# Inverse decay by a second scan and a Newton step, and one projection moved, in an RWKV-7 / HGRN-2 / attention trunk

## The chip, the cores and the metric

The kernel runs on one core of a Trainium2 chip. The metric is the device time of one execution in microseconds (us), as the median of several executions. The engines are named PE (TensorE, matrix products; PEld is its weight load), DVE (VectorE), ACT (ScalarE), POOL (GpSimd) and SP (SyncE, which here issues most DMAs). Each runs its own list of instructions in a fixed order and waits for the others through semaphores. SBUF is the on-chip memory that all of them read; PSUM is the small memory that PE writes its sums to.

## The reference

One layer of a hybrid trunk on 1024 tokens of width 1024, in fp32: a normed input projection `w_in`, three groups of heads (HGRN2, dilated window attention, RWKV-7), an output projection, a gated MLP with a short convolution, an embedding gate and a last norm. The change lies in RWKV-7 alone:

```python
w = -jax.nn.softplus(-(w0 + jnp.tanh(wd) @ w2)) - 0.5
decay = jnp.exp(-jnp.exp(w))          # = exp(-e^-0.5 * sigmoid(w0 + tanh(wd) @ w2))
a = jax.nn.sigmoid(a0 + ad @ a2)
kk = kk / jnp.maximum(jnp.linalg.norm(kk, axis=-1, keepdims=True), 1e-12)
k = k * (1.0 + (a - 1.0) * k_a)
# over the tokens t, per head of 64:
sa = state @ (-kk_t)
state = state * w_t + sa (kk_t * a_t)^T + v_t k_t^T
y_t = state @ r_t
```

The recurrence is computed in chunks of 64 tokens. Within a chunk `gam` is the running product of the decay and `ig` its inverse; r and kk are multiplied by `gam`, k and kk*a by `ig`, after which a chunk is a few matrix products and the inverse of a triangular matrix.

## The kernel before

Rows (partitions) are channels, columns are the 1024 tokens. A projection of 128 channels is 48 matmuls of 128x128 by 512 columns: 8 parts of the contraction, three products of high and low halves each (hi*hi, hi*lo, lo*hi, L137, L139, L141), two halves of the tokens. Its sum `dp` takes one of the **two** PSUM buffers of the pool `dps` (2 x 1024 columns). A third projection can start only when the first one's buffer has been read for the last time. Its weights come by DMA as `wraw`, ACT casts `whi` (L114), and POOL or DVE by turns subtracts `wlo` (L116).

There are 30 projections j. 0 to 7 are RWKV's (lora, gate, then k, r, v of head pair 0 as 2, 3, 4, of pair 1 as 5, 6, 7) and run through `proj` and `mix_in` (L492): scale `dp` in place by the norm (L320, DVE), copy on ACT (L501), mix with the previous token (L502, DVE). 8 and up belong to the other heads and are the **filling**: `project_rest` (L425) is a generator that issues 6 matmuls at each step, at a tile's end its finish (DVE scale L320 and ACT sigmoid L457 by halves, or one DVE product L454, into `zst`) and its store.

The heads are worked in two pairs p. For each:

- `rwkv_prep` (L537): k, its squares and norm (`kks`, `kr`), the LoRA products `lo`, sigmoids for w and a, an exp (L572), the scan for `gam` (L581), the reciprocal `ig` (L584), `ai`, r, `kkn`, `bhat`, `ar` (L609, L622), 8 or 6 filling steps, then `rwkv_scores` (PE `sc` L654, DVE `sc` L656), for pair 1 also v, then k with a, `khat` (POOL, L623), `bv`.
- `rwkv_inverse` (L660): 31 steps of two small DVE operations, `Tt` (L678) and `Tb` (L680), and DMAs that lay the result out as Tc and Uc. PE meanwhile does filling, v of pair 0, and the bonus `bon`; then it needs Tc for `py` (L790).
- `rwkv_main`: 22 slots of small matmuls (`px`, `pgm`, `pyo`, `pS`), one filling step in each; the state S passes from chunk to chunk by pS and DVE L903. `rwkv_norm` of the first half runs as a member of it (gnv, gnr on POOL, y times gnr, L764), of the second half behind it, with transposes `yt` (L770) and `pg`.

The order of the program text is not the order on the engines: the framework's scheduler orders the instructions of each engine by the dependencies and its own costs, and the buffers of the pools add waits. What stands below as the order is the built program's.

Of the kernel before, what the change touches and what calls it, by code (L numbers as in the profile page):

```python
# [18 lines left out]
P = 128  # L19
# [70 lines left out]
class Trunk:  # L90
# [334 lines left out]
    def project_rest(self, js):  # L425


        nc = self.nc
        w = None
        for i, j in enumerate(js):  # L430
            w = w or self.load_w(self.a["w_in"][j])
            ps = self.dps.tile([P, T], F32, tag="dp", name=self.nm("dp"))
            nxt = None
            for k in range(ND):
                self.mm3({0: ps[:, :HT], 1: ps[:, HT:]}, w(k), self.X[k], k == 0, k == ND - 1)
                if k == 3 and i + 1 < len(js):
                    nxt = self.load_w(self.a["w_in"][js[i + 1]])
                yield
            w = nxt
            t = self.keep.tile([P, T], F32, tag="zst", name=self.nm("zst"), bufs=2)  # L440
            kind = (j - 8) % 4 if j < 24 else 2
            parts = [(t, ps, self.R)]
            if j < 24 and kind < 3:
                parts = [(t[:, :HT], ps[:, HT:][:, ::-1], self.R[:, HT:][:, ::-1]), (t[:, HT:], ps[:, :HT], self.R[:, :HT])]
            for part in parts:
                self.finish(kind, *part)
            d = self.zpool.tile([P, T], F32, tag=f"z{j}", name=f"z{j}")
            nc.sync.dma_start(d, t)
            self.z[j] = d
        yield  # L450
# [55 lines left out]
    def rwkv(self):  # L506
# [7 lines left out]
        for p in (0, 1):  # L514
            d = {}
            lead, n = self.FILL[p]
            fill = self.project_rest([next(js) for _ in range(n)])
            with tc.tile_pool(name=f"pre{p}", bufs=1) as tp:
                self.rwkv_prep(p, tp, lt, d, fill)
                self.rwkv_inverse(p, tp, d)  # L520
# [16 lines left out]
    def rwkv_prep(self, p, tp, lt, d, fill):  # L537
# [6 lines left out]
        def col(c):  # L544
            return par[:, c + p:c + p + 1]
# [18 lines left out]
        for hf in (0, 1):  # L564
# [3 lines left out]
            nc.scalar.activation(w[:, sl], ps, AF.Sigmoid, bias=col(PC_W0))  # L568
            ps = mxp.tile([P, HT], F32, tag="mx", name=self.nm("lo"))
            nc.tensor.matmul(ps, par[64:128, PC_LORA + p * P:PC_LORA + (p + 1) * P], lt[64:128, sl], start=True, stop=True)  # L570
            nc.scalar.activation(a[:, sl], ps, AF.Sigmoid, bias=col(PC_A0))
        nc.scalar.activation(w, w, AF.Exp, scale=-EXP_M05)  # L572

        dz = tr("dz")
        w3 = w.rearrange("p (c i) -> p c i", i=64)
        dz3 = dz.rearrange("p (c i) -> p c i", i=64)
        nc.gpsimd.memset(dz, 0.0)
        nc.vector.tensor_copy(dz3[:, :, 0:1], w3[:, :, 0:1])
        nc.vector.memset(w3[:, :, 0:1], 0.0)
        gam = tr("gam")  # L580
        nc.vector.tensor_tensor_scan(gam, w, dz, 0.0, ALU.mult, ALU.add)  # L581
        ig = tr("ig")
        for hf in (0, 1):
            nc.vector.reciprocal(ig[:, hf * HT:(hf + 1) * HT], gam[:, hf * HT:(hf + 1) * HT])  # L584
        ai = tr("ai")
        nc.vector.tensor_tensor(ai, a, ig, ALU.mult)
        r = self.mix_in(3 + 3 * p, 0 + p, "r", tr)
# [21 lines left out]
            nc.vector.tensor_tensor(a4[:, :, :, 1:], k4[:, :, :, 1:], g4[:, :, :, :63], ALU.mult)  # L609
            nc.scalar.copy(a4[:, :, :, 0:1], k4[:, :, :, 0:1])  # L610
        d.update(ar=ar, be=be, kh=kh)
        for _ in range(6 if p else 8):
            next(fill)
        self.rwkv_scores(p, tp, d)
        if p:
# [115 lines left out]
    HALVES = tuple((slice(a, a + 32), slice(a + 32, a + 64)) for a in (0, 64))  # L731

    def rwkv_norm(self, p, sg, d, hf, fill, n):
        for i, _ in enumerate(self.rwkv_norm_steps(p, sg, d, hf)):
            for _ in range(2 if i < 4 else 1):
                for _ in range(1 if n == 3 else 2):
                    next(fill, None)

    def rwkv_norm_steps(self, p, sg, d, hf):

# [25 lines left out]
        yield  # L766
        yield
        pt = mxp.tile([P, HT], F32, tag="mx", name=self.nm("yt"))
        for m in range(4):
            nc.tensor.transpose(self.turned(pt[:, m * P:(m + 1) * P], m % 2), y[:, m * P:(m + 1) * P], self.ident)  # L770
        nc.vector.tensor_scalar(o, pt, col(PC_LNW), col(PC_LNB), ALU.mult, ALU.add)
        nc.vector.tensor_tensor(o, o, d["bv"][:, sl], ALU.add)
        pg = mxp.tile([P, HT], F32, tag="mx", name=self.nm("pg"))
# [1086 lines left out]
```

## Time and profile before

| | us |
|---|---|
| median of 3 executions | 1405.99 (1405.21 to 1406.52) |
| the profiled execution | 1404.77 |
| its span, first to last instruction | 1403.0 |
| PE busy in the span | 1375.7 |
| mean granted PE clock | 0.994 of full speed |

In the timeline a row is: start in us from the span's start, duration, engine, line, operation, out<-in, shapes, xcount (rows of one group in a row), and in brackets the idle time of the engine ahead of it with what ended it. A row of waits gives engine, what waited, <- what ended the wait: us in total, how often, the longest. A row of stretches gives the stretch, its length, the busy time (and count) of PE, PEld, DVE, ACT and POOL, the PE clock, the DMA share and GB/s. Pair 0's preparation runs from about 53 to 89 us, its inverse to 124, the first loop from 133 to 190, pair 1's preparation from 210 to 254, its inverse to 286, the second loop from there.

### The profile page before, as it was taken

What the parts mean: (1) busy time and instruction counts of PE and PEld (TensorE: products, weight loads), DVE (VectorE), ACT (ScalarE), POOL (GpSimd) and SP (SyncE); (2) the same over time, 40 slices, a digit from 0 to 9 for tenths busy, and PEclk for the clock granted to TensorE, in tenths of its full rate; (3) what the DMA queues carried; (4) which work ended last, traced back from release to release, by engine and by line L of the source; (5) the groups of instructions that cost most, each with busy time, mean ns of one, the idle gap of its engine ahead of it and who ended that gap; (6) DMA issues with size and microseconds to landing.
All of it is one profiled execution on the core that took longest, in us unless ns stands there. A gap on an engine that the chain in (4) does not pass through costs nothing.

```text
span 1403.0 us, 22344 instructions
## 1 busy us (share of the span) xinstructions
PE 1375.7 (98%) x8644; PEld 1116.5 (80%) x8644; DVE 1063.7 (76%) x1613; ACT 611.8 (44%) x1049; POOL 395.5 (28%) x287
## 2 busy tenths in 40 slices
PE   9999999999999999999999999999999999999997
PEld 6878777877878768788788888888888888888886
DVE  7696456835667796468889888888988799777685
ACT  7522323133255584255544343444344444455542
POOL 5411012101222242221345454545453000002342
PEclk9999999999999999999999999999999999999998
DMA  6123111321622212653232332332324963441443
GB/s 224 61 83 104 64 61 47 100 73 62 225 83 99 91 61 71 253 180 125 94 127 98 113 103 90 102 105 98 114 98 166 351 217 106 127 143 45 136 138 140
DMA packets 80122, 167.61 MB, mean 119 GB/s; under 512 B 19984, under 2 KB 22288, under 8 KB 80016
## 3 DMA queue, kind: packets, MB, share of 16 engines
q1 hardware_dynamic: 66784, 147.05, 31.3%
q10 hardware_dynamic: 12224, 15.47, 3.2%
q0 software_dynamic: 1008, 3.67, 0.7%
q8 instruction: 68, 1.11, 0.3%
q14 instruction: 38, 0.31, 0.1%
HBM read 119.76 MB, written 46.40 MB: 118 GB/s over the span
## 4 chain that ended last, share of the span: by engine, by line
PE 78%; DVE 8%; issue 8%; ACT 3%; POOL 3%; DMA 1%; SPq 0%; POOLq 0%; ACTq 0%; DVEq 0%
PE bg L1338 17%; PE bv L1338 13%; PE bv L1639 7%; PE bg L1639 7%; PE dp L137 7%; PE dp L139 7%; PE dp L141 7%; PE swq L1169 1%; DVE ig L584 1%; PE hsc L1015 1%; PE zp L137 1%; DVE xl L409 1%; PE zp L141 1%; PE zp L139 1%; PE swo L1209 1%
## 5 line engine op out<-in xcount | busy, mean ns | idle before, releaser
L137 PE MATMUL dp<-xh,whi 128*128 128x512 f32 x544 | 186.9, 406 | 1.2 <-DVE r L502 0.7
L139 PE MATMUL dp<-xl,whi 128*128 128x512 f32 x544 | 180.5, 394 | 0.6 <-DVE xl L409 0.5
L141 PE MATMUL dp<-xh,wlo 128*128 128x512 f32 x544 | 179.7, 392 | 0.0
L116 POOL TENSOR_TENSOR wlo<-wraw,whi 128x512 fp32r<-128x512 f32 x60 | 84.5, 1410 | 264.9 <-ACT whi L114 226.8
L116 POOL TENSOR_TENSOR wlo<-raw,whi 128x512 fp32r<-128x512 f32 x84 | 135.0, 1626 | 75.9 <-ACT whi L114 75.9
L114 ACT CAST whi<-wraw 128x512 fp32r<-128x512 f32 x120 | 72.9, 618 | 158.0 <-PE dp L139 103.0
L1338 PE MATMUL bg<-t,whi 128*128 128x512 f32 x352 | 133.4, 389 | 0.0
L139 PEld LDWEIGHTS dp<-xl,whi 128*128 128x128 f32 x544 | 102.3, 188 | 24.6 <-DVE xl L409 2.5
L141 PEld LDWEIGHTS dp<-xh,wlo 128*128 128x128 f32 x544 | 102.2, 188 | 23.8 <-issue 2.0
L137 PEld LDWEIGHTS dp<-xh,whi 128*128 128x128 f32 x544 | 98.8, 189 | 26.0 <-issue 3.9
L116 POOL TENSOR_TENSOR wlo<-s,whi 128x512 fp32r<-128x512 f32 x44 | 64.5, 1466 | 168.6 <-ACT whi L114 168.6
L1639 PE MATMUL bg<-t,whi 128*128 128x512 f32 x308 | 95.2, 390 | 0.0
L1639 PE MATMUL bv<-t,whi 128*128 128x512 f32 x308 | 94.8, 389 | 0.0
L114 ACT CAST whi<-raw 128x512 fp32r<-128x512 f32 x88 | 52.7, 620 | 93.7 <-issue 48.5
L114 ACT CAST whi<-s 128x512 fp32r<-128x512 f32 x66 | 38.9, 620 | 120.2 <-PE bg L1338 112.8
L1338 PEld LDWEIGHTS bg<-t,whi 128*128 128x128 f32 x352 | 66.1, 188 | 13.7
L190 POOL TENSOR_TENSOR rst<-rst,mhalf 128x4 f32<-128x4 f32 (+1 forms) x9 | 10.2, 1134 | 234.0 <-DVE rst L186 218.0
L1635 ACT CAST t<-t 128x512 fp32r<-128x512 f32 x77 | 47.8, 622 | 45.8 <-PE bv L1639 32.7
L1338 PE MATMUL bg<-t,wlo 128*128 128x512 f32 x176 | 67.5, 389 | 0.0
L1639 PEld LDWEIGHTS bv<-t,whi 128*128 128x128 f32 x308 | 57.8, 188 | 12.0
L1639 PEld LDWEIGHTS bg<-t,whi 128*128 128x128 f32 x308 | 57.8, 188 | 11.9
L116 DVE TENSOR_TENSOR wlo<-wraw,whi 128x512 fp32r<-128x512 f32 x60 | 48.2, 807 | 20.7 <-ACT whi L114 18.5
(417 smaller groups left out, 3423.6 us busy)
## 6 DMA issues: line engine op xcount, KB each, us to landing
raw<-in_ffn_up_dram SPq DMA_DIRECT2D x44, 512.0 KB, 3.5
wraw<-in_w_in_dram SPq DMA_DIRECT2D x28, 512.0 KB, 3.4
z<-zst SPq DMA_DIRECT2D x18, 512.0 KB, 2.9
gb<-ct SPq DMA_DIRECT2D x33, 256.0 KB, 2.3
t<-gb SPq DMA_DIRECT2D x33, 256.0 KB, 2.7
t<-gt SPq DMA_DIRECT2D x33, 256.0 KB, 2.7
zl<-z SPq DMA_DIRECT2D x16, 512.0 KB, 4.4
wraw<-in_ple_gate_dram SPq DMA_DIRECT2D x16, 512.0 KB, 3.4
```

Of the source, the lines that this page charges most:

```text
L114: self.cast = nc.scalar.copy(hi, src).ins
L116: eng.tensor_tensor(lo, src, hi.bitcast(F32), ALU.subtract)
L137: nc.tensor.matmul(ps[hf], wh, xh[hf], start=first, stop=False)
L139: nc.tensor.matmul(ps[hf], wh, xl[hf], start=False, stop=False)
L141: self.step = nc.tensor.matmul(ps[hf], wl, xh[hf], start=False, stop=last).ins
L409: nc.vector.scalar_tensor_tensor(lo, x, g[:, k:k + 1], hi.bitcast(F32), ALU.mult, ALU.subtract)
L584: nc.vector.reciprocal(ig[:, hf * HT:(hf + 1) * HT], gam[:, hf * HT:(hf + 1) * HT])
L1015: nc.tensor.matmul(sc[g:g + 64, c, :], ks[:, c * P + g:c * P + g + 64], x, start=True, stop=True)
L1169: m = nc.tensor.matmul(pq[h][:, b:b + w], d["q"][hs, qb * P:nk], d["k"][hs, b:b + w], start=True, stop=True)
L1338: nc.tensor.matmul(ps, w[part == 2][:, s], X[k][part == 1], start=start and k == part == 0, stop=k == 3 and part == 2, skip_group_check=no ...
L1635: nc.scalar.copy(xh, x)
L1639: nc.tensor.matmul(ps[m], wt[part == 2][:, m * P:(m + 1) * P], (xh, xl)[part == 1], start=k == part == 0, stop=k == NK - 1 and part == 2)
```

## The change

It has four parts.

1. `ig` is no longer a reciprocal of `gam`. A second exp with the opposite sign and a second scan build the running product of the inverse decays, and a Newton step x(2 - gam x) corrects it with two scalar_tensor_tensor.
2. In pair 1 the sigmoid of the second half of a is issued behind the exps.
3. Projection 5 (pair 1's k) is the ninth of the first loop's filling; its PSUM tile is kept and `mix_in` finds it.
4. 9 and 7 filling steps instead of 8 and 6 are taken ahead of the scores, and the transposes `yt` of pair 0's second half are issued behind the fifth filling step of the norm.

```diff
--- before.py
+++ after.py
@@ -437,6 +437,9 @@
                     nxt = self.load_w(self.a["w_in"][js[i + 1]])
                 yield
             w = nxt
+            if j < 8:
+                self.early[j] = ps
+                continue
             t = self.keep.tile([P, T], F32, tag="zst", name=self.nm("zst"), bufs=2)
             kind = (j - 8) % 4 if j < 24 else 2
             parts = [(t, ps, self.R)]
@@ -514,7 +517,7 @@
         for p in (0, 1):
             d = {}
             lead, n = self.FILL[p]
-            fill = self.project_rest([next(js) for _ in range(n)])
+            fill = self.project_rest([next(js) for _ in range(n)] + [5] * (p == 0))
             with tc.tile_pool(name=f"pre{p}", bufs=1) as tp:
                 self.rwkv_prep(p, tp, lt, d, fill)
                 self.rwkv_inverse(p, tp, d)
@@ -568,20 +571,26 @@
             nc.scalar.activation(w[:, sl], ps, AF.Sigmoid, bias=col(PC_W0))
             ps = mxp.tile([P, HT], F32, tag="mx", name=self.nm("lo"))
             nc.tensor.matmul(ps, par[64:128, PC_LORA + p * P:PC_LORA + (p + 1) * P], lt[64:128, sl], start=True, stop=True)
-            nc.scalar.activation(a[:, sl], ps, AF.Sigmoid, bias=col(PC_A0))
-        nc.scalar.activation(w, w, AF.Exp, scale=-EXP_M05)
+            if not (p and hf):
+                nc.scalar.activation(a[:, sl], ps, AF.Sigmoid, bias=col(PC_A0))
+        gam = tr("gam")
+        nc.scalar.activation(gam, w, AF.Exp, scale=EXP_M05)
+        m = nc.scalar.activation(w, w, AF.Exp, scale=-EXP_M05)
+        if p:
+            with self.tc.issue_after(m.ins):
+                nc.scalar.activation(a[:, sl], ps, AF.Sigmoid, bias=col(PC_A0))
 
         dz = tr("dz")
-        w3 = w.rearrange("p (c i) -> p c i", i=64)
         dz3 = dz.rearrange("p (c i) -> p c i", i=64)
         nc.gpsimd.memset(dz, 0.0)
-        nc.vector.tensor_copy(dz3[:, :, 0:1], w3[:, :, 0:1])
-        nc.vector.memset(w3[:, :, 0:1], 0.0)
-        gam = tr("gam")
-        nc.vector.tensor_tensor_scan(gam, w, dz, 0.0, ALU.mult, ALU.add)
         ig = tr("ig")
-        for hf in (0, 1):
-            nc.vector.reciprocal(ig[:, hf * HT:(hf + 1) * HT], gam[:, hf * HT:(hf + 1) * HT])
+        for src, dst in ((gam, ig), (w, gam)):
+            s3 = src.rearrange("p (c i) -> p c i", i=64)
+            nc.vector.tensor_copy(dz3[:, :, 0:1], s3[:, :, 0:1])
+            nc.vector.memset(s3[:, :, 0:1], 0.0)
+            nc.vector.tensor_tensor_scan(dst, src, dz, 0.0, ALU.mult, ALU.add)
+        nc.vector.scalar_tensor_tensor(w, gam, -1.0, ig, ALU.mult, ALU.mult)
+        nc.vector.scalar_tensor_tensor(ig, w, 2.0, ig, ALU.add, ALU.mult)
         ai = tr("ai")
         nc.vector.tensor_tensor(ai, a, ig, ALU.mult)
         r = self.mix_in(3 + 3 * p, 0 + p, "r", tr)
@@ -609,7 +618,7 @@
             nc.vector.tensor_tensor(a4[:, :, :, 1:], k4[:, :, :, 1:], g4[:, :, :, :63], ALU.mult)
             nc.scalar.copy(a4[:, :, :, 0:1], k4[:, :, :, 0:1])
         d.update(ar=ar, be=be, kh=kh)
-        for _ in range(6 if p else 8):
+        for _ in range(7 if p else 9):
             next(fill)
         self.rwkv_scores(p, tp, d)
         if p:
@@ -731,10 +740,15 @@
     HALVES = tuple((slice(a, a + 32), slice(a + 32, a + 64)) for a in (0, 64))
 
     def rwkv_norm(self, p, sg, d, hf, fill, n):
+        steps = 0
+        self.before = None
         for i, _ in enumerate(self.rwkv_norm_steps(p, sg, d, hf)):
             for _ in range(2 if i < 4 else 1):
                 for _ in range(1 if n == 3 else 2):
                     next(fill, None)
+                    steps += 1
+                    if p == 0 and steps == 5:
+                        self.before = self.step
 
     def rwkv_norm_steps(self, p, sg, d, hf):
 
@@ -766,8 +780,11 @@
         yield
         yield
         pt = mxp.tile([P, HT], F32, tag="mx", name=self.nm("yt"))
-        for m in range(4):
-            nc.tensor.transpose(self.turned(pt[:, m * P:(m + 1) * P], m % 2), y[:, m * P:(m + 1) * P], self.ident)
+        with ExitStack() as order:
+            if hf and self.before:
+                order.enter_context(self.tc.issue_after(self.before))
+            for m in range(4):
+                nc.tensor.transpose(self.turned(pt[:, m * P:(m + 1) * P], m % 2), y[:, m * P:(m + 1) * P], self.ident)
         nc.vector.tensor_scalar(o, pt, col(PC_LNW), col(PC_LNB), ALU.mult, ALU.add)
         nc.vector.tensor_tensor(o, o, d["bv"][:, sl], ALU.add)
         pg = mxp.tile([P, HT], F32, tag="mx", name=self.nm("pg"))
```

**Order on the engines, pair 0 around the scores, DVE.** Names: `k`, `ar`, `sc`, `bv` as above, `dp_619` / `dp_623` the first filling tile (j = 8), `wlo` weights. Before:

```order
L620 SCALAR_TENSOR_TENSOR k_466<-ka_719,k_466 128x1024
L656 TENSOR_TENSOR sc_678<-sc_679,cst 128x4x64
L656 TENSOR_TENSOR sc_678<-sc_680,cst 128x4x64
L656 TENSOR_TENSOR sc_678<-sc_699,cst 128x4x64
L656 TENSOR_TENSOR sc_678<-sc_700,cst 128x4x64
L622 TENSOR_TENSOR ar_601<-r_577,gam_510 128x4x128
L622 TENSOR_TENSOR ar_601<-r_577,gam_510 128x4x2x64
L627 SCALAR_TENSOR_TENSOR bv_727<-r_577,par,k_466 128x1024
L320 TENSOR_TENSOR dp_619<-dp_619,rstd 128x512
L116 TENSOR_TENSOR wlo_923<-wraw_915,whi_921 128x512
L116 TENSOR_TENSOR wlo_987<-wraw_983,whi_985 128x512
L320 TENSOR_TENSOR dp_619<-dp_619,rstd 128x512
```

With the change:

```order
L629 SCALAR_TENSOR_TENSOR k_466<-ka_737,k_466 128x1024
L320 TENSOR_TENSOR dp_623<-dp_623,rstd 128x512
L631 TENSOR_TENSOR ar_605<-r_581,gam_505 128x4x128
L631 TENSOR_TENSOR ar_605<-r_581,gam_505 128x4x2x64
L665 TENSOR_TENSOR sc_696<-sc_697,cst 128x4x64
L665 TENSOR_TENSOR sc_696<-sc_698,cst 128x4x64
L665 TENSOR_TENSOR sc_696<-sc_717,cst 128x4x64
L320 TENSOR_TENSOR dp_623<-dp_623,rstd 128x512
L665 TENSOR_TENSOR sc_696<-sc_718,cst 128x4x64
L636 SCALAR_TENSOR_TENSOR bv_745<-r_581,par,k_466 128x1024
L116 TENSOR_TENSOR wlo_927<-wraw_919,whi_925 128x512
```

The scale of the first filling tile's first half moved ahead of the products for ar, and the second half's stands among the sc; before, both stood behind all of these.

**Pair 0, PE, around the start of v** (`dp_850` before, `dp_860` now; `dp_827` / `dp_689` is the second filling tile, `bon` the bonus). In brackets are the semaphores on which a row waits; Activation is ACT. Before:

```order
L141 MATMUL dp_827<-xh_119,wlo_652 128x512
L141 MATMUL dp_827<-xh_103,wlo_652 128x512
L635 MATMUL bon_1029<-bv_727,cst 128x512 [waits DVE_49,PE_49]
L635 MATMUL bon_1032<-bv_727,cst 128x512 [waits PE_49]
L137 MATMUL dp_850<-xh_105,whi_842 128x512 [waits Activation_49]
L137 MATMUL dp_850<-xh_89,whi_842 128x512
```

With the change:

```order
L139 MATMUL dp_689<-xl_110,whi_650 128x512
L139 MATMUL dp_689<-xl_94,whi_650 128x512
L141 MATMUL dp_689<-xh_109,wlo_652 128x512
L141 MATMUL dp_689<-xh_93,wlo_652 128x512
L137 MATMUL dp_860<-xh_105,whi_852 128x512 [waits PE_49,Activation_49]
L137 MATMUL dp_860<-xh_89,whi_852 128x512
L139 MATMUL dp_860<-xl_106,whi_852 128x512
```

v now starts behind 12 matmuls of the second filling tile and waits for ACT there; its other 30 matmuls, and the bonus later still, follow v. What ACT has to have done is the last read of dp_623, whose buffer dp_860 takes.

**Pair 1, DVE, behind v's projection** (`dp_2361` / `dp_2375` is v, `dp_2263` / `dp_2271` the filling tile, whose finish is `zst`). Before:

```order
L320 TENSOR_TENSOR dp_2361<-dp_2361,rstd 128x1024
L627 SCALAR_TENSOR_TENSOR bv_2422<-r_2221,par,k_2117 128x1024
L502 SCALAR_TENSOR_TENSOR v_2411<-dp_2361,par,v_2411 128x1023
L454 TENSOR_TENSOR zst_2527<-dp_2263,rstd 128x1024
L678 TENSOR_TENSOR Tt_2434<-At_2426,Tb_2431 64x31
L636 TENSOR_TENSOR bv_2422<-v_2411,bon_2578 128x512
```

With the change:

```order
L320 TENSOR_TENSOR dp_2375<-dp_2375,rstd 128x1024
L687 TENSOR_TENSOR Tt_2448<-At_2440,Tb_2445 64x31
L457 TENSOR_TENSOR zst_2535<-dp_2271,rstd 128x1024
L505 SCALAR_TENSOR_TENSOR v_2425<-dp_2375,par,v_2425 128x1023
L636 SCALAR_TENSOR_TENSOR bv_2436<-r_2229,par,k_2121 128x1024
L689 TENSOR_TENSOR Tb_2445<-Tb_2445,Tt_2448 64x31
```

The finish of the filling tile moved ahead of v's mix and bv, and the inverse's first Tt ahead of it.

## The prediction

> **What bounds the kernel now.** I read the page first (busy shares, chain), then the busy time by stretches of the span, then PE's waits from 40 to 300 us, where the edited code runs, then the order of time around each wait.
>
> ```profile
> PE 1375.7 (98%) x8644; PEld 1116.5 (80%) x8644; DVE 1063.7 (76%) x1613; ACT 611.8 (44%) x1049; POOL 395.5 (28%) x287
> ...
> 40.00:135.00 95.00, 94.03 (x565) 76.25 (x565) 70.76 (x115) 31.99 (x44) 21.23 (x15) 1.00 0.26 78
> 135.00:205.00 70.00, 67.70 (x966) 51.19 (x965) 36.72 (x95) 24.00 (x65) 7.98 (x6) 1.00 0.20 70
> 205.00:300.00 95.00, 93.22 (x651) 74.24 (x650) 61.91 (x108) 24.16 (x37) 16.15 (x12) 1.00 0.25 75
> ```
>
> PE (second number of a stretch) is the bound. In these 260 us, which hold nearly all that the change touches, it idles 0.97 + 2.30 + 1.78 = 5.1 us. PE's amount of work does not change, so 5.1 us, 0.4% of the span, is about the most that the change can gain; what it can lose is new waits of PE. These are the waits there:
>
> ```profile
> PE yt L770 <- DVE y L764: 1.6, 1, 1.6
> ...
> PE dp L137 <- DVE r L502: 0.7, 1, 0.7
> ...
> 290.32 0.24 PE L790 MATMUL py<-Tc,sc 32*32 32x32 f32 x2
> ...
> 290.96 1.19 PE L790 MATMUL py<-Tc,sc 32*32 32x32 f32 x62
> ```
>
> With the split py, in which PE stands about 0.7 us for the second part of Tc (290.96 against 290.32), they are 0.8 in pair 0 (the first sc) and 1.65 + 0.70 + 0.56 + 0.69 = 3.6 us in pair 1: 4.4 us in all.
>
> **Pair 0: decay and inverse decay.** Removed: two reciprocals. Added on DVE: a copy and a memset, a second scan, two steps of scalar_tensor_tensor.
>
> ```profile
> 60.81 2.29 DVE L581 TENSOR_TENSOR_SCAN gam<-w,dz 128x1024 f32<-128x1024 f32 x1
> 63.02 1.21 DVE L320 TENSOR_TENSOR dp<-dp,rstd 128x1024 f32<-128x1024 f32 x1
> 64.14 6.55 DVE L584 RECIPROCAL ig<-gam 128x512 f32<-128x512 f32 x2
> 70.73 1.23 DVE L586 TENSOR_TENSOR ai<-a,ig 128x1024 f32<-128x1024 f32 x1
> ...
> 76.17 1.27 DVE L609 TENSOR_TENSOR ar<-kkn,gam 128x504 f32<-128x504 f32 x2
> 77.36 1.22 DVE L620 SCALAR_TENSOR_TENSOR k<-ka,k 128x1024 f32<-128x1024 f32 x1
> 78.50 1.41 DVE L656 TENSOR_TENSOR sc<-sc,cst 128x256 f32<-128x256 f32 x4
> 82.14 1.27 DVE L627 SCALAR_TENSOR_TENSOR bv<-r,par,k 128x1024 f32<-128x1024 f32 x1
> 83.34 0.69 DVE L320 TENSOR_TENSOR dp<-dp,rstd 128x512 f32<-128x512 f32 x1
> ...
> 59.28 1.06 ACT L572 ACTIVATE w<-w 128x1024 f32<-128x1024 f32 x1
> 84.06 0.60 ACT L457 ACTIVATE zst<-dp 128x512 f32<-128x512 f32 x1 [0.34 <-DVE dp L320]
> ```
>
> The new exp stands first on ACT and takes the old one's place (59.28), the old one ends 1.06 later, while the first scan runs. So: scan 60.81, dp L320 63.02, copy and memset (0.37, the space ahead of the first scan), scan 64.5, first step 66.7, second 67.9, ai 69.1 (1.14 us from one such step to the next, as k to sc), against 70.73: 1.6 us earlier. But POOL has work there:
>
> ```profile
> 61.46 2.74 POOL L116 TENSOR_TENSOR wlo<-wraw,whi 128x512 fp32r<-128x512 f32 x1 [2.54 <-ACT whi L114]
> 69.01 1.30 POOL L116 TENSOR_TENSOR wlo<-wraw,whi 128x512 fp32r<-128x512 f32 x1 [4.81 <-ACT whi L114]
> 78.66 2.41 POOL L623 TENSOR_TENSOR khat<-k,ig 128x1024 f32<-128x1024 f32 x1 [8.35 <-DVE k L620]
> ...
> L622 DVE TENSOR_TENSOR ar<-r,gam x4: 678/683/1792, 79.8 to 242.0; 128x512 f32<-128x512 f32 x4
> ...
> 737.84 4.02 POOL L116 TENSOR_TENSOR wlo<-raw,whi 128x512 fp32r<-128x512 f32 x2
> 738.92 1.79 DVE L1459 TENSOR_TENSOR s<-s,raw 128x512 f32<-128x512 f32 x1
> ```
>
> Read together, these say that POOL and a DVE instruction with two inputs in SBUF exclude each other and take turns: wlo at 61.46 needed 2.74 us (1.3 otherwise) and ended 1.1 after the scan; the ar of r and gam at 79.8 took 1.79 instead of 0.68, with khat on POOL; at 738.92 a DVE step right behind another lost 1.1 us to a POOL step already waiting. The reciprocal is not hit: wlo at 69.01 ran inside it at 1.30. In the changed program the same wlo finds the second step and then ai. It is waiting when ai's turn comes, so ai goes at 70.3: 0.4 us earlier, not 1.6. The first wlo costs nothing, since dp L320, with its first input in PSUM, covers it. I take 0.4 and keep 1.6 as the other bound.
>
> [...]
>
> **Pair 0: PE.**
>
> ```profile
> 75.78 0.39 PE L139 MATMUL dp<-xl,whi 128*128 128x512 f32 x1
> 77.00 1.52 PE L654 MATMUL sc<-ar,bhat 64*64 64x64 f32 x64 [0.83 <-DVE ar L609]
> 78.45 0.50 PE L139 MATMUL dp<-xl,whi 128*128 128x512 f32 x1
> ...
> 87.44 1.88 PE L635 MATMUL bon<-bv,cst 128*128 128x512 f32 x4
> ```
>
> Despite the ninth filling step asked for, the built order has 54 projection matmuls between kkb and sc, before it had 57; one is 0.23 us (78.45 to 87.44 holds 39). PE reaches sc at 75.78 + 0.39 - 0.69 = 75.5; sc can go 0.83 after ar starts: 75.8 + 0.83 = 76.6. Wait 1.1 us, before 0.83.
>
> Behind sc the order is now 12 matmuls of the second fill tile and then v at once; before 39, the bonus, and only then v. v's tile takes the PSUM buffer of the first fill tile, which is free when ACT has finished zst's second half. On DVE this hangs behind k, half a scale, ar(r,gam) twice and three sc. khat holds the first ar(r,gam) as before, so that pair ends 82.14 - 76.17 = 5.97 after ar starts; three sc steps add 1.0 (four in 1.32); ACT's half ends 1.32 after DVE's half starts (83.34 to 84.66). Together 8.3 after ar: 75.8 + 8.3 = 84.1. PE is there at 76.6 + 1.45 + 12 x 0.23 = 80.8. **New wait: 3.3 us**, before covered by 39 matmuls and the bonus. If khat let ar(r,gam) pass (k 2.3 after ar, half a scale 0.6, twice ar 1.2, then the same 1.0 and 1.3: 82.2) it would be 1.5. Pair 0: 1.1 + 3.3 - 0.83 = **+3.6**; bounds +0.7 (khat harmless, no wait at sc: 1.5 - 0.83) and +3.6. Next comes py behind the inverse:
>
> ```profile
> 89.61 1.29 DVE L678 TENSOR_TENSOR Tt<-At,Tb 64x31 f32<-64x31 f32 x1
> 122.61 1.12 DVE L682 COPY Ub<-Tb 64x1024 f32<-64x1024 f32 x1
> ...
> 284.60 1.12 DVE L682 COPY Ub<-Tb 64x1024 f32<-64x1024 f32 x1
> ```
>
> The inverse took 33.0 us (to 122.61), and py's second part could start 6.4 after such an end (284.60 to 290.96). Now it begins behind v's scale, 1.2 after v's end, so Tc is there at 40.6 from v's end; PE gets to py 180 matmuls (41.4) and the bonus (1.8) after v's end, at 43.2. Margin 2.6 us: no wait.
>
> **The first loop.** The norm of the first half is on the path to S at the loop's end:
>
> ```profile
> 178.91 0.69 DVE L764 TENSOR_TENSOR y<-y,gnr 128x512 f32<-128x512 f32 x1 [1.76 <-POOL gnr L763]
> 181.18 0.70 DVE L886 TENSOR_TENSOR MG<-pgm,ar 128x128 f32<-128x128 f32 x2 [0.39 <-ACT N L884]
> 182.13 0.22 PE L790 MATMUL pS<-S,MG 64*64 64x64 f32 x1
> ```
>
> zst (1.2) moves between reduce and scale of gnv, and a POOL wlo now follows gnr and can hold y for 1.1. A wlo of 0.6 leaves the space between y and MG. MG at 181.88 + 1.2 + 1.1 - 0.6 = 183.6 would leave pS (182.13) waiting 1.4; nothing if DVE's gap of 1.76 takes it up. I take **+0.8**.
>
> **Pair 1.**
>
> ```profile
> 222.37 2.29 DVE L581 TENSOR_TENSOR_SCAN gam<-w,dz 128x1024 f32<-128x1024 f32 x1
> 232.29 1.21 DVE L586 TENSOR_TENSOR ai<-a,ig 128x1024 f32<-128x1024 f32 x1
> 238.55 1.52 PE L654 MATMUL sc<-ar,bhat 64*64 64x64 f32 x64 [0.56 <-DVE ar L609]
> 252.57 1.21 DVE L454 TENSOR_TENSOR zst<-dp,rstd 128x1024 f32<-128x1024 f32 x1
> 221.91 1.28 ACT L571 ACT_TABLE_LOAD   x1
> ```
>
> The delayed sigmoid of a changes nothing: the built order had its table load (221.91) behind the exp already. The keys' projection only changes place: its 48 matmuls run before yt, which is why yt's wait (1.65) goes; its cover is gone in front of kks, where 18 matmuls of r (4.1 us), yt and pg stand against four steps in a row on DVE and ACT of 1.1 to 1.3 each: I take 0.1. DVE: scan 222.37, wlo 0.6, copy and memset, scan 225.7 to 228.0, step, scale, step: ai at 231.5, 0.8 earlier. The POOL wlo that follows r's last matmul comes at about 225.7, behind the second scan's start, and takes 1.25 from the first step: 0.45 later. sc: PE arrives at 238.55 - 0.70 - 0.56 + 0.23 + 0.1 = 237.6 (the wait on r is gone, 72 matmuls for 71); ar lets it go at 238.55 + 0.45 = 239.0: 1.4 us (0.1 without POOL). Behind v only 6 matmuls (1.36) are left of the fill tile, and the next tile needs that buffer: v's scale (1.1 as at 63.02), the first Tt and zst (1.21) stand before it, 2.7 with the start: 1.4 us. py: 174 matmuls and the bonus as before plus the two waits: none. Pair 1: 0.1 + 1.4 + 1.4 - 3.6 = **-0.7** (-2.0 without POOL). In the second loop gnr's y is no longer held: **-0.2**.
>
> Sum: 3.6 + 0.8 - 0.7 - 0.2 = **+3.5 us**; bounds 0.7 + 0 - 2.0 - 0.2 = -1.5 and 3.6 + 1.4 - 0.7 + 0 = +4.3. The profiled execution (1404.77, span 1403.0) would come to 1408.3; it lies 1.2 under the median of 1405.99, so the forecast is 1409.5.
>
> **Rivals.** *No change:* POOL loses the turns, or the new steps are not held. Then ai gains its 1.6 and 0.8: pair 0 3.2 - 0.83 = 2.4, pair 1 -1.9, the loop as above: +1.1, 1407.1. For it: the margin by which wlo (69.01) is ahead of ai (69.1) is small. Against: POOL's turns at 738 us. *Faster:* the PSUM buffer is no limit, v starts without a wait, since the release comes earlier than I place it, and the four old waits go: -4.4, 1401.6. It needs zst's second half before 80 us, 4 us before my date, so DVE would have to take it ahead of ar(r,gam), against the built order. *Slower still:* the inverse, with more fill steps woven into it, takes 2 us beyond its margin (37.6 instead of 33.0) and py of pair 0 waits for Tc: 3.5 + 2 = +5.5, 1411.5; for it, a margin of only 2.6 us in 43; against, what delays v delays both sides alike. That the scan and Newton step move nothing, being covered, is the middle of the no-change case.
>
> **Numbers.** A difference under 0.2%, 2.8 us, cannot be told from none. Forecast +3.5 0.45 and py 0.05, so slower 0.50; no change 0.37; faster 0.13. The range leaves out most of the faster case and the end of the py case: 1403.0 to 1411.0; the forecast's own is 1408 to 1411.
>
> **What would show it.** On PE: a wait of 3.3 at v's first dp L137 behind sc, released by ACT zst; sc waiting about 1.1 and 1.4; a wait of 1.4 on DVE zst behind pair 1's v; no yt, r or py wait. On DVE: ai stretched to about 2.4 us in pair 0, a Newton step in pair 1. If v's wait is absent, the main term is wrong, and with it the sign.

## The result and the profile after

The changed kernel is slower. Its median is 1410.83 us (1410.1 to 1412.36, 6 runs) against 1405.70 us (1404.8 to 1406.52, 6 runs) for the kernel before on the same chip: a ratio of 1.0039 with a 95% interval of 1.0028 to 1.0050, or +5.1 us where +3.5 was forecast. In two later comparisons the same program came to +7.5 and +7.9 us (below).

The profiled execution took 1410.1 us with a span of 1408.3. The first rows are from its page and from its busy time by stretches of the span, in the columns explained above.

```profile
PE 1375.6 (98%) x8644; PEld 1116.8 (79%) x8644; DVE 1061.6 (75%) x1619; ACT 613.7 (44%) x1051; POOL 396.5 (28%) x287
...
0.00:40.00 40.00, 36.01 (x139) 25.95 (x140) 31.28 (x40) 26.40 (x46) 22.76 (x23) 0.96 0.61 211
40.00:135.00 95.00, 90.73 (x490) 73.25 (x489) 69.58 (x117) 31.37 (x42) 19.54 (x14) 1.00 0.24 71
135.00:205.00 70.00, 69.30 (x1032) 52.90 (x1031) 33.32 (x91) 25.06 (x67) 9.75 (x7) 1.00 0.23 74
205.00:300.00 95.00, 91.46 (x549) 73.39 (x548) 62.99 (x112) 23.64 (x35) 17.92 (x12) 1.00 0.27 81
300.00:360.00 60.00, 58.98 (x923) 44.31 (x922) 29.39 (x86) 21.10 (x61) 5.46 (x4) 1.00 0.17 57
```

PE works as long as before (1375.6 against 1375.7 us), so all of the difference is idle time of PE. Two rows of before are needed beside those that the prediction showed, for the start and for the stretch from 300 us:

```profile
0.00:40.00 40.00, 37.29 (x144) 26.96 (x145) 30.94 (x40) 26.84 (x47) 23.04 (x24) 0.96 0.62 216
...
300.00:360.00 60.00, 59.71 (x830) 45.45 (x829) 33.14 (x87) 19.75 (x58) 8.75 (x6) 1.00 0.18 63
```

| stretch, us | PE idle before | after | difference |
|---|---|---|---|
| 0 to 40 (start) | 2.71 | 3.99 | +1.3 |
| 40 to 135 (pair 0) | 0.97 | 4.27 | +3.3 |
| 135 to 205 (first loop) | 2.30 | 0.70 | -1.6 |
| 205 to 300 (pair 1) | 1.78 | 3.54 | +1.8 |
| 300 to 360 (second loop) | 0.29 | 1.02 | +0.7 |
| 360 to the end | 19.3 | 19.2 | -0.1 |

The spans differ by 5.3 us: 1.3 from the start, which nothing in the change touches, and 4.1 from 40 us on. PE's waits between 40 and 320 us, in the profile after:

```profile
PE sc L663 <- DVE ar L618: 3.4, 4, 1.8
PE dp L137 <- ACT zst L460: 2.9, 1, 2.9
PE dp L137 <- DVE zst L457: 1.5, 1, 1.5
PE pyo L807 <- DVE S L920: 0.4, 1, 0.4
PE pS L807 <- DVE MG L903: 0.2, 1, 0.2
```

The waits on y (yt) and on r that stood there before are gone, and so is the split py. In their place stand two waits on `zst`, the buffer waits of the forecast, and longer waits of the scores. The timeline of pair 0 shows where the largest comes from:

```profile
67.40 1.23 DVE L592 SCALAR_TENSOR_TENSOR w<-gam,ig 128x1024 f32<-128x1024 f32 x1
...
68.66 1.23 DVE L593 SCALAR_TENSOR_TENSOR ig<-w,ig 128x1024 f32<-128x1024 f32 x1
...
69.59 1.44 POOL L116 TENSOR_TENSOR wlo<-wraw,whi 128x512 fp32r<-128x512 f32 x1 [4.83 <-ACT whi L114]
...
69.92 2.20 DVE L595 TENSOR_TENSOR ai<-a,ig 128x1024 f32<-128x1024 f32 x1
...
76.34 1.27 DVE L618 TENSOR_TENSOR ar<-kkn,gam 128x504 f32<-128x504 f32 x2
...
77.17 0.34 PE L663 MATMUL sc<-ar,bhat 64*64 64x64 f32 x8 [1.10 <-DVE ar L618]
...
77.76 1.04 PE L663 MATMUL sc<-ar,bhat 64*64 64x64 f32 x56 [0.25 <-DVE ar L618]
...
78.83 2.40 POOL L632 TENSOR_TENSOR khat<-k,ig 128x1024 f32<-128x1024 f32 x1 [7.80 <-DVE k L629]
...
79.27 3.11 DVE L631 TENSOR_TENSOR ar<-r,gam 128x512 f32<-128x512 f32 x2
...
83.30 0.69 DVE L320 TENSOR_TENSOR dp<-dp,rstd 128x512 f32<-128x512 f32 x1
...
84.02 0.60 ACT L460 ACTIVATE zst<-dp 128x512 f32<-128x512 f32 x1 [4.02 <-DVE dp L320]
...
84.67 0.73 PE L137 MATMUL dp<-xh,whi 128*128 128x512 f32 x2 [2.92 <-ACT zst L460]
```

Read it from the bottom. PE stands 2.92 us before v's first matmul because ACT has not yet read the last half of the PSUM buffer that v takes over. ACT waits for the DVE scale at 83.30, and that stands behind `ar` of r and gam, which took 3.11 us beside `khat` on POOL. Above it one sees that the second scan and the Newton step end at 69.9, 0.8 us ahead of the old reciprocals (64.14 + 6.55), that `ai` then loses 1.0 us to POOL's wlo, and that `ar` starts at 76.34 against 76.17 before: no gain is left. In pair 1 a Newton step itself is hit:

```profile
228.17 2.95 POOL L116 TENSOR_TENSOR wlo<-wraw,whi 128x512 fp32r<-128x512 f32 x1 [5.20 <-ACT whi L114]
...
230.07 2.13 DVE L592 SCALAR_TENSOR_TENSOR w<-gam,ig 128x1024 f32<-128x1024 f32 x1
...
241.20 0.34 PE L663 MATMUL sc<-ar,bhat 64*64 64x64 f32 x8 [1.80 <-DVE ar L618]
...
241.79 1.04 PE L663 MATMUL sc<-ar,bhat 64*64 64x64 f32 x56 [0.25 <-DVE ar L618]
...
256.81 0.72 PE L137 MATMUL dp<-xh,whi 128*128 128x512 f32 x2 [1.49 <-DVE zst L457]
```

The step took 2.13 us where the same one took 1.23 in pair 0.

### The profile page after: what moved, and what is told of

Its sections match the earlier page's. It is cut to its first block, busy times and chain, and to the rows that moved or that the text cites. A ratio compares the mean times of both kernels' runs of the same rounds, so it can differ in the third digit from the quotient of the medians.

```text
span 1408.3 us, 22351 instructions
## 1 busy us (share of the span) xinstructions
PE 1375.6 (98%) x8644; PEld 1116.8 (79%) x8644; DVE 1061.6 (75%) x1619; ACT 613.7 (44%) x1051; POOL 396.5 (28%) x287
## 4 chain that ended last, share of the span: by engine, by line
PE 80%; DVE 5%; issue 3%; POOL 2%; ACT 2%; DMA 0%; POOLq 0%; ACTq 0%; DVEq 0%
PE bg L1355 17%; PE bv L1355 13%; PE bv L1656 7%; PE dp L137 7%; PE bg L1656 7%; PE dp L139 7%; PE dp L141 7%; PE swq L1186 1%; PE hsc L1032 1%; PE zp L137 1%; PE swo L1226 1%; PE swt L1212 1%; PE zp L141 1%; PE zp L139 1%; PE sk L807 1%
## 5 line engine op out<-in xcount | busy, mean ns | idle before, releaser
L116 DVE TENSOR_TENSOR wlo<-wraw,whi 128x512 fp32r<-128x512 f32 x60 | 48.3, 806 | 19.2 <-ACT whi L114 19.2
```

The costliest lines, as they stand in the source:

```text
L116: eng.tensor_tensor(lo, src, hi.bitcast(F32), ALU.subtract)
```

## The experiments

The theory under test: the scan and Newton step gain nothing, moving the keys gains, and the loss is the new waits of PE, above all those for a PSUM buffer, which come from where the ninth and seventh filling steps leave a tile unfinished and from v's early place. Rivals: the arithmetic itself costs the time; the start of the program does; something that the waits don't show does. The runs came in four groups (e1 to e4, e5 to e8, e9 to e11, e12 and e13). Each group ran with the kernel before on its own chip, whose medians were 1405.87, 1405.19, 1405.62 and 1405.20 us; each run is compared with its own.

| run | edit | median, us | ratio to before (95%) |
|---|---|---|---|
| e1_v_later | v five filling steps later | 1407.31 | 1.0014 (1.0005 to 1.0023) |
| e2_eight_fills_pair1 | 9 and 8 filling steps | 1408.26 | 1.0023 (1.0014 to 1.0031) |
| e3_khat_on_dve | khat on DVE | 1409.21 | 1.0024 (1.0015 to 1.0032) |
| e4_fills_8_6 | 8 and 6 filling steps as before | 1412.56 | 1.0049 (1.0036 to 1.0061) |
| e5_reciprocal_back | reciprocals in place of scan and Newton | 1406.75 | 1.0013 (1.0004 to 1.0022) |
| e6_newton_alone | before, with scan and Newton only | 1410.61 | 1.0038 (1.0025 to 1.0052) |
| e7_keys_alone | before, with the keys moved only | 1403.15 | 0.9986 (0.9977 to 0.9995) |
| e8_best | v later, 10 and 8 filling steps | 1402.70 | 0.9979 (0.9970 to 0.9988) |
| e9_before_again | none, kernel before | 1405.44 | 1.0000 (0.9991 to 1.0009) |
| e10_change_again | none, changed kernel | 1413.16 | 1.0057 (1.0045 to 1.0069) |
| e11_best_with_reciprocal | e8 with reciprocals | 1402.30 | 0.9978 (0.9970 to 0.9987) |
| e12_wait_filled | idle matmuls in the wait | 1411.67 | 1.0044 (1.0030 to 1.0057) |
| e13_change_beside | none, beside e12 | 1413.07 | 1.0055 (1.0042 to 1.0068) |

### The waits for a PSUM buffer

**e1_v_later**

```diff
-                if p == 0 and i == 1:
+                if p == 0 and i == 6:
                     d["v"] = self.mix_in(4, 4, "v")
```

> The changed kernel with one number altered: pair 0's v is projected five filling steps later, after the second filling tile is complete instead of inside it. Theory (v's first matmul waits for the PSUM buffer of the first filling tile, and this is lost PE time): the wait of 2.92 us on ACT zst is gone, nothing takes its place, and the time falls by 2.9 us from 1410.8 to about 1407.9. Rival A (the wait only moves, to py behind the inverse, since v is mixed later): PE waits about 2 to 3 us at py, time stays at 1410 to 1411. Rival B (most of the loss lies in the first 40 us, where PE idled 1.3 us more): 1409.5 or more.

1407.31 us (1406.90 to 1409.55, 11 runs). The wait on ACT zst is gone from the profile; sc (3.4) and DVE zst (1.5) stay. With v moved the change costs 1.4 us instead of 5.1 or more: at least the whole wait comes back, and nothing else takes its place.

**e2_eight_fills_pair1**

```diff
-        for _ in range(7 if p else 9):
+        for _ in range(8 if p else 9):
```

> The changed kernel with 8 instead of 7 filling steps ahead of pair 1's scores, so that the filling tile is complete before v and its buffer is free when the next one starts. Theory: pair 1's wait on DVE zst (1.49) is gone and the wait of sc (1.80 + 0.25) falls by one filling step, 1.36 us, to about 0.7: -2.85 us, 1408.0; if the inverse, which now stands behind bv and v's mix, makes py wait about 1 us, 1408.9. Rival (the scores set the pace: what PE does not wait for at zst it waits for at py): py waits 2.8, time unchanged at 1410.8.

1408.26 us (1406.70 to 1412.59, 11 runs). With eight steps, a whole tile, ahead of pair 1's scores, the second buffer wait is gone and sc falls from 3.4 to 2.1.

**e3_khat_on_dve**

```diff
-        nc.gpsimd.tensor_tensor(kh, k, ig, ALU.mult)
 ...
         nc.vector.scalar_tensor_tensor(bv, r, col(PC_RK), k, ALU.mult, ALU.mult)
+        nc.vector.tensor_tensor(kh, k, ig, ALU.mult)
```

> The changed kernel with khat computed by DVE behind bv instead of by POOL. Theory (POOL's khat holds the first product for ar up, and with it the scale that stands behind it and frees v's PSUM buffer): the two products take 1.3 us instead of 3.11, v's wait falls by 1.8 from 2.92 to 1.1, and the time by up to 1.8 to 1409.0, less what khat's 1.2 us on DVE cost the inverse of pair 1. Rival (it is the order on DVE alone, POOL does not matter): products and wait as before, 1410.8.

1409.21 us (1407.10 to 1410.28, 11 runs). The two products of r and gam, and then v's wait, from this run's timeline and waits:

```profile
79.52 1.27 DVE L631 TENSOR_TENSOR ar<-r,gam 128x512 f32<-128x512 f32 x2
```

```profile
PE dp L137 <- ACT zst L460: 1.1, 1, 1.1
```

1.27 us instead of 3.11, and a wait of 1.1 instead of 2.9: `khat` on POOL is what made v's wait so long. The buffer's late release is the cause of the wait, and `khat` 1.8 us of its size.

**e4_fills_8_6**

```diff
-        for _ in range(7 if p else 9):
+        for _ in range(6 if p else 8):
```

> The changed kernel with 8 and 6 filling steps ahead of the scores, as before the change; all else as changed. The built order then has v of pair 0 behind the whole second filling tile and the bonus, and in pair 1 twelve matmuls and the bonus behind v. Theory (the added filling step makes both new waits on PSUM buffers): both waits (2.92, 1.49) are gone, sc waits 1.36 longer in each pair (2.7 and 3.4): -4.4 + 2.7 = -1.7, 1409.1. Rival (the added step is what it was meant for, and pays): slower than the changed kernel by 2.7, 1413.5.

1412.56 us (1410.61 to 1413.88, 5 runs), over the expected 1409.1. Its waits:

```profile
PE sc L663 <- DVE ar L618: 6.1, 4, 3.2
PE py L807 <- DMA Tc<-Tz: 1.4, 2, 1.0
```

Both buffer waits are gone, and sc has grown to 6.1 as expected. What was not expected is the wait of py on Tc, and a clock granted at about half (the number behind POOL's count) behind the waits of sc and of py in pair 1, which is taken up below. From the stretches of 2 us:

```profile
242.00:244.00 2.00, 2.00 (x6) 1.52 (x6) 1.52 (x4) 0.00 (x0) 0.00 (x0) 0.53 0.12 47
...
300.00:302.00 2.00, 2.00 (x15) 1.19 (x14) 0.00 (x0) 1.59 (x3) 0.00 (x0) 0.52 0.63 262
```

The rival's figure of some 1413 is nearer, but by other means than it gave. So the added filling steps of the change are not the mistake by themselves: without them nothing is gained (1.0049 here, 1.0039 to 1.0057 for the changed kernel). In pair 1 the mistake is their number against the tile's eight (e2), in pair 0 the place of v (e1).

### The arithmetic and the keys

**e5_reciprocal_back**

```diff
-        nc.scalar.activation(gam, w, AF.Exp, scale=EXP_M05)
 ...
-        for src, dst in ((gam, ig), (w, gam)):
+        for src, dst in ((w, gam),):
 ...
-        nc.vector.scalar_tensor_tensor(w, gam, -1.0, ig, ALU.mult, ALU.mult)
-        nc.vector.scalar_tensor_tensor(ig, w, 2.0, ig, ALU.add, ALU.mult)
+        for hf in (0, 1):
+            nc.vector.reciprocal(ig[:, hf * HT:(hf + 1) * HT], gam[:, hf * HT:(hf + 1) * HT])
```

> The changed kernel with the two reciprocals back in place of the second exp, the second scan and the Newton step; the rest as changed. Theory (POOL's turns eat the Newton step's gain, and its cost is the order that it brings on DVE): the products for ar start only 0.4 us later in pair 0 and 0.4 earlier in pair 1; the built order now has the filling tile's scale ahead of the products that khat holds, so v's wait shrinks from 2.9 to about 0.2; sc waits about 1.1 and 1.6. -3.4 us, 1407.4. Rival (the Newton step saves the 1.6 and 0.8 us that its instructions are shorter): slower than the changed kernel, 1411 to 1413.

1406.75 us (1405.56 to 1409.72, 11 runs). From its timeline:

```profile
70.96 1.23 DVE L594 TENSOR_TENSOR ai<-a,ig 128x1024 f32<-128x1024 f32 x1
...
76.41 1.27 DVE L617 TENSOR_TENSOR ar<-kkn,gam 128x504 f32<-128x504 f32 x2
...
77.60 0.69 DVE L320 TENSOR_TENSOR dp<-dp,rstd 128x512 f32<-128x512 f32 x1
```

`ai` ends at 72.2 and `ar` starts at 76.41, with Newton 72.1 and 76.34: the same. But the built order is another one. The scale of the tile whose buffer v needs (77.60) now comes ahead of k and of the products of r, and v does not wait at all. The difference of the two arithmetics in this program therefore lies mainly in the order that the scheduler made of each, not in the instructions' time; e11 below tries this again in another order.

**e6_newton_alone** is the kernel before with the second exp, the second scan and the Newton step, and nothing else.

```diff
+        nc.scalar.activation(gam, w, AF.Exp, scale=EXP_M05)
 ...
-        for hf in (0, 1):
-            nc.vector.reciprocal(ig[:, hf * HT:(hf + 1) * HT], gam[:, hf * HT:(hf + 1) * HT])
+        for src, dst in ((gam, ig), (w, gam)):
 ...
+        nc.vector.scalar_tensor_tensor(w, gam, -1.0, ig, ALU.mult, ALU.mult)
+        nc.vector.scalar_tensor_tensor(ig, w, 2.0, ig, ALU.add, ALU.mult)
```

> The kernel before with the second exp, the second scan and the Newton step alone. Theory: ar 0.4 us earlier in pair 0 and 0.4 later in pair 1; the built order has 48 instead of 57 matmuls ahead of sc in pair 0 and 91 instead of 94 in pair 1, so sc waits about 2.7 and 2.0; yt's wait stays. 1.9 + 1.4 = +3.3 us against before, 1409.2. Rival (a shorter chain on DVE is a gain by itself): 1404 to 1405.

1410.61 us (1410.00 to 1414.12, 5 runs), slower by 5.4. Here too the order is another: PE arrives early at pair 0's scores and stands there.

```profile
74.07 0.61 PE L141 MATMUL dp<-xh,wlo 128*128 128x512 f32 x2
77.16 2.37 PE L656 MATMUL sc<-ar,bhat 64*64 64x64 f32 x64 [2.47 <-DVE ar L611]
...
80.47 1.05 PE L139 MATMUL dp<-xl,whi 128*128 128x512 f32 x2
```

After the wait of 2.47 us the 64 small matmuls took 2.37 us instead of 1.52, and pairs of large ones 1.05 instead of 0.62: PE was granted half its clock there, from 76.7 to 83.5 us. The profiled execution, 1414.12 us, is the longest of the five.

**e7_keys_alone** is the kernel before with only projection 5 in the filling.

```diff
+            if j < 8:
+                self.early[j] = ps
+                continue
 ...
-            fill = self.project_rest([next(js) for _ in range(n)])
+            fill = self.project_rest([next(js) for _ in range(n)] + [5] * (p == 0))
```

> The kernel before with pair 1's keys in the first loop's filling alone. Theory: yt's wait (1.65) goes, the wait on r (0.70) turns into a longer wait of sc (1.3), 0.1 is lost at kks: -1.5 us against before, 1404.4. Rival (PE just meets the next wait that much earlier): no change, 1405.9.

1403.15 us (1401.53 to 1405.11, 11 runs), 2.0 faster than before. The waits on y and on r are gone, as in the changed kernel, and the scores (sc) wait 2.2 instead of 1.4. This part of the change is a gain by itself, although its profile has a half clock of 3.4 us behind the wait of 1.33 us at pair 1's scores.

### A mended order

**e8_best** keeps all four parts of the change, and sets v four filling steps later (the expectation says five; it is four) and the filling steps to 10 and 8.

```diff
-                if p == 0 and i == 1:
+                if p == 0 and i == 5:
 ...
-        for _ in range(7 if p else 9):
+        for _ in range(8 if p else 10):
```

> The changed kernel with 10 and 8 filling steps ahead of the scores and pair 0's v five filling steps later than its first place, behind the complete second filling tile. Theory: pair 0's wait on ACT zst (2.92) and its sc wait (1.35) are gone, pair 1's wait on DVE zst (1.49) is gone and sc waits 0.7 instead of 2.05: -7.1 us, 1403.7, 0.15% under the kernel before. Rival (with fewer waits ahead, PE is at py before the inverse): py waits 2 to 3 us in one or both pairs, 1405 to 1407.

1402.70 us (1399.65 to 1403.30, 11 runs): faster than both kernels. The largest waits left:

```profile
PE py L807 <- DMA Tc<-Tz: 1.0, 1, 1.0
PE sc L663 <- DVE ar L618: 0.7, 2, 0.5
```

**e11_best_with_reciprocal** is e8 with the reciprocals of e5.

> The version of e8 (10 and 8 filling steps, v behind the complete second tile) with the reciprocals back. Theory (scan and Newton step gain nothing on the path that PE waits for): sc waits 0 to 0.4 in pair 0 and at most what it did in e8 in pair 1, time as e8 within 0.7 us of 1402.7. Rival (once the order is mended, the shorter inverse decay pays 1 us or more): 1403.7 or more.

1402.30 us (1400.63 to 1403.30, 11 runs), a ratio of 0.9978 against 0.9979 for e8 (each to the kernel before on its chip). Where the order is right, it is all one whether `ig` is made by reciprocals or by scan and Newton step.

### What the waits don't show

The waits account for 4.1 us from 40 us on; the medians differ by 5.1, and in later comparisons by more. Four runs ask where the rest is. **e9_before_again** and **e10_change_again** are the two kernels once more, unchanged, on one chip.

> The kernel before, unaltered, for a second profile. In the first 40 us, which the change leaves alone, PE idled 2.67 us in the profile of before and 3.98 in that of the changed kernel. Theory (this stretch differs from run to run, by when the first inputs land): here it idles 3.5 to 4.5, and the waits behind it are those of the first profile (sc 1.4, yt 1.6, r 0.7). Rival (the changed kernel loses 1.3 there): 2.7 again.

> The changed kernel, unaltered, for a second profile and a narrower interval. Theory (the change costs what PE waits more from 40 us on, 3.7 us between the first two profiles): 3.7 us over before on this chip, 0.26%. Rival (it costs 5.1, as the first medians say): 0.36%.

e9 came to 1405.44 us (1404.04 to 1406.48, 11 runs), e10 to 1413.16 us (1410.43 to 1415.03, 6 runs): +7.5, more than either figure expected. The start is no part of it. In this execution of the kernel before PE idled 4.23 us in the first 40:

```profile
0.00:40.00 40.00, 35.77 (x136) 25.83 (x137) 30.93 (x40) 25.96 (x46) 21.77 (x23) 0.96 0.60 210
```

That is what the changed kernel did there (3.99, and 4.21 in e10), so the first profile of before had a short start by chance. The waits of e10 are those of the first profile after, to the tenth. The clock is not. PE's timeline behind v's wait, in e10, and two stretches there, which meet where the granted clock changes:

```profile
84.82 0.72 PE L137 MATMUL dp<-xh,whi 128*128 128x512 f32 x2 [2.90 <-ACT zst L460]
...
86.00 1.05 PE L141 MATMUL dp<-xh,wlo 128*128 128x512 f32 x2
```

```profile
82.25:85.66 3.41, 0.84 (x4) 0.71 (x5) 3.41 (x8) 0.60 (x1) 0.17 (x2) 1.00 0.11 44
85.66:89.07 3.41, 3.41 (x10) 2.63 (x9) 0.60 (x1) 0.00 (x0) 0.00 (x0) 0.50 1.00 341
```

From 85.66 to 89.07 us the granted clock is half and PE is busy throughout. The loss is half of 3.41 us: 1.7 us. PE's busy time in the whole span rises with it, from 1375.6 to 1377.6 us, and e10's profiled execution is 2.4 us longer than the first one after (1412.46 against 1410.1). The first profile after has no such stretch there (the last section shows it). So the same waits are followed by a half clock in one execution and not in another.

**e12_wait_filled** fills v's wait: behind pair 0's scores PE runs 24 more matmuls of 128x128 by 256 columns, into the unused half of a score tile. Their result is read by nobody; nothing of the computation is left out. **e13_change_beside** is the changed kernel beside it.

```diff
-            ps = [mxp.tile([P, 4, 64], F32, tag="mx", name=self.nm("sc")) for _ in (0, 1)]
+            ps = [mxp.tile([P, 8, 64], F32, tag="mx", name=self.nm("sc")) for _ in (0, 1)]
 ...
+            if g and not p:
+                x = self.X[0][0][0]
+                for _ in range(24):
+                    nc.tensor.matmul(ps[1].rearrange("p c i -> p (c i)")[:, 256:], x[:, :P], x[:, :256], start=True, stop=True)
 ...
```

> The changed kernel with 24 useless matmuls (128x128 by 256 columns, into an unused half of a score tile, about 0.11 us each, 2.7 us in all) behind pair 0's scores, so that PE works through most of the wait of 2.92 us that v meets. Nothing that v waits for moves. Theory (the wait costs more than its length: in some executions PE's granted clock falls to half for some 3.4 us behind it, which costs another 1.7 us, as in the profile of e10 at 84 to 90 us): the wait shrinks to about 0.2, no clock dip follows it, the median falls by 1 to 2 us against the unaltered change beside it and the spread narrows. Rival (a wait costs its length only): median and spread as those of the unaltered change.

> The changed kernel, unaltered, beside e12 on the same chip. Theory: 1411 to 1413.5, with executions up to 1415, 1 to 2 us over e12. Rival: equal to e12 within 0.5 us.

e12: 1411.67 us (1410.83 to 1413.53, 5 runs); e13: 1413.07 us (1411.25 to 1414.45, 5 runs). From e12's timeline and its stretches:

```profile
80.37 3.12 PE L667 MATMUL sc<-xh 128*128 128x256 f32 x24
...
86.31 0.73 PE L137 MATMUL dp<-xh,whi 128*128 128x512 f32 x2
```

```profile
242.00:244.00 2.00, 0.88 (x28) 0.81 (x32) 2.00 (x4) 0.00 (x0) 1.09 (x2) 0.87 0.00 0
244.00:246.00 2.00, 2.00 (x50) 1.79 (x43) 2.00 (x4) 0.00 (x0) 0.00 (x0) 0.50 0.03 8
```

v starts as long behind the first score matmul as without the filling (7.5 us in both), PE is not idle ahead of it, and the clock stays whole there. Pair 1's wait of 1.8 us for the scores, which was not filled, has a half clock behind it in this very execution, its longest. With useless work in the place of idle time the median is 1.4 us lower, about the price of one such stretch. The ranges overlap and there are five runs of each, so this points to the clock but does not prove it. The mean clock on record for each execution points the same way. Of 17 executions of the changed kernel (the first comparison, e10 and e13) the five at 0.990 or 0.991 took 1413.07 to 1415.03 us, the seven at 0.994 or 0.995 took 1410.10 to 1412.74, and none of 97 executions of the kernel before (the four groups and e9) was granted less than 0.993. That a half clock came behind such waits is shown (3.41 us in e10); how often, and whether it makes up all of the 1 to 4 us that the waits leave, is open.

## Why the prediction was right and wrong

The direction and the mechanism were right, the size was too small.

- **v's wait in pair 0** was forecast as 3.3 and measured as 2.92, released by ACT zst as said; e1 took it away and at least 3.7 us came back (+1.4 instead of +5.1 in the first comparison), more than the wait itself. That `khat` holds the products of r and gam was right as well (e3: 1.8 us). The scores' wait was forecast as 1.1; it was 1.10, and a second piece of 0.25 which came because sc now starts when the first of the two halves of `ar` is there. Pair 0 came to +3.3 (forecast +3.6).
- **The scan and Newton step** were to bring `ai` 0.4 us earlier in pair 0. It ended at 72.12, against 70.73 + 1.23 = 71.96 before. The forecast that POOL eats the gain was right: `ai` took 2.20 us (about 2.4 forecast).
- **POOL against the Newton step.** The prediction had no row of a scalar_tensor_tensor against POOL. That such a step would be held was the author's estimate, from the rows of tensor_tensor and of the scan. There is a row now: 2.13 us instead of 1.23 beside a wlo that took 2.95 (pair 1), so this step lost 0.9 us beside POOL.
- **First loop**: forecast +0.8, measured about 0: the stretch gained 1.6, which is yt's wait alone (1.65). The term itself came nearly as forecast. zst stands ahead of gnv's scale, y was held by POOL (1.77 us beside two wlo that took 2.97 in all), and the new waits of pyo (0.42) and pS (0.20) make 0.6 (two rows are below). What the prediction left out is the wait of sk on S in this loop, 0.65 us before, which is no longer there.
- **Pair 1**: forecast -0.7. Stretch 205 to 300 gives +1.8, and with yt's 1.65, which the prediction booked here, +0.1. The wait on zst was 1.49 (1.4 forecast), and the waits on yt, r and py are gone. Two terms had the wrong size. The scores' wait was 1.80 + 0.25 = 2.05 instead of 1.4. The split py, taken as a wait of 0.69 that would go, was mostly not idle: a matmul of pt ran between its two parts (290.50 us), and PE idled 0.23 us in all from 290 to 292.5 us before.
- **Second loop**: forecast -0.2, measured +0.6 from 300 us on. The trace has a new wait of sk on S there, 0.6 us, while a wait of that size stays in the first loop (sk before, pyo 0.4 and pS 0.2 now); where it comes from was not tried.

The two rows of the first loop, in the profile after: zst took 1.28 us ahead of gnv's scale, and y took 1.77 where it took 0.69 before.

```profile
182.43 1.28 DVE L457 TENSOR_TENSOR zst<-dp,rstd 128x512 f32<-128x512 f32 x2
...
185.55 1.77 DVE L778 TENSOR_TENSOR y<-y,gnr 128x512 f32<-128x512 f32 x1 [1.76 <-POOL gnr L777]
```

The terms so add up to +4.1 where +3.5 was forecast. That they come so near is partly luck: pair 0 and the first loop came out 0.3 and 0.8 lower, pair 1 and the second loop about 0.8 each higher.

The step that failed is the one from this sum to the time, "The profiled execution (1404.77, span 1403.0) would come to 1408.3": it took PE's idle time for the whole cost. The prediction allowed nothing for the granted clock behind a new wait, and its upper bound of +4.3 was made of waits alone, where +5.1 was measured. e10, e4, e6 and e12 show stretches of half clock behind new waits, of which e10's costs 1.7 us. In the first comparison the remainder is 1.0 us, in the two later ones 3.4 and 3.8; that the clock makes up all of it is not shown. The profile of before had a hint of it, elsewhere in the program, where both kernels have the same wait:

```profile
511.21 1.06 PE L1049 MATMUL vt<-cst,hk 128*128 128x128 f32 x4 [2.44 <-ACT hV L1044]
```

```profile
511.33:514.74 3.41, 3.41 (x36) 2.98 (x36) 3.26 (x7) 3.21 (x5) 2.16 (x2) 0.50 0.54 148
```

The rivals: *no change* (1407.1) fell since POOL did take its turns (`ai` 2.20 us, a Newton step 2.13) and v did wait (2.92). *Faster* (1401.6) fell with v's wait; e8 is what it would have looked like. *Slower still* (1411.5) gave nearly the measured time, but by a wait of py that isn't there, as the one row of py in pair 0 shows (no bracket, so no idle time ahead of it):

```profile
138.34 1.20 PE L807 MATMUL py<-Tc,sc 32*32 32x32 f32 x64
```

## What to carry to other kernels

A tile whose work is moved ahead takes a buffer, and the buffer's last reader may hang on an engine's queue far behind the place that looked free: look for that reader before moving anything, and put whole tiles, not pieces, ahead of a projection that needs one of two PSUM buffers (with 10 and 8 steps and v later the kernel was 0.21% faster than before, with 9 and 7 it was 0.4 to 0.6% slower). An operation made faster on paper gains nothing while another engine's turn (1.0 us of `ai` here) or a scheduler's new order takes it back; here reciprocal and Newton step are worth the same once the order is right. And a new wait of 1.3 to 3.2 us beside a run of small matmuls cost more than its length in some executions here, since PE's clock was halved for 3.4 us behind it (1.7 us in e10).

## What was not expected of the hardware

The clock was granted at half for 3.4 us behind waits of PE of 1.33 us (e7), 1.8 (e12, pair 1), 2.47 (e6, there for 6.8 us), 2.90 (e10) and 3.2 (e4), and in e4 once more behind py's waits of 1.4 in all; small matmuls (the scores, py) ran right behind the wait each time but in e10, where the scores had ended 3.0 us ahead of it. It did not happen behind the same waits in every execution: the profiles of after, e2 and e13 have the wait of 2.9 and no half clock there. In e10 the stretch costs 1.7 us.

The traces suggest why it comes and goes. Within an execution the half-clock stretches start whole multiples of 3.413 us apart: 9.57 and 511.33 us in before (147 of them), 8.08 and 516.67 in after (149), 76.72 and 243.97 in e6 (49), 12.25 and 517.43 in e13 (148). So in these executions the clock changed on a grid of 3.413 us, and the grid lay differently against the program in each. In e10 the 3.41 us ahead of the half clock, 82.25 to 85.66, held 2.57 us of idle PE. In after a grid line fell inside the same wait, at 83.17:

```profile
79.76:83.17 3.41, 1.99 (x9) 1.31 (x7) 3.41 (x5) 0.23 (x1) 2.49 (x3) 1.00 0.00 0
83.17:86.58 3.41, 1.92 (x8) 1.61 (x9) 2.93 (x5) 0.60 (x1) 0.00 (x0) 1.00 0.42 171
```

The two stretches idled 1.42 and 1.49 us, and no half clock followed either; in e13 it was 1.67 and 1.24, and none followed. How much idle time is enough is not settled: in e7 a wait of 1.33 us, with the 64 small matmuls of the scores (1.52 us) behind it, was followed by the half clock, and in before the 0.99 us that PE idled from 6.16 to 9.57 us. Nor was PE idle throughout the stretch ahead: it was busy for 0.84 us (e10) and 2.42 us (before, 6.16 to 9.57) of the 3.41. The two stretches of before:

```profile
6.16:9.57 3.41, 2.42 (x8) 0.95 (x7) 1.39 (x3) 2.37 (x5) 1.65 (x3) 1.00 0.97 311
9.57:12.98 3.41, 3.30 (x8) 2.21 (x9) 3.16 (x4) 3.41 (x7) 2.83 (x3) 0.50 1.03 379
```
